# A decoder trunk step on one core: the samples' attention spread over other stages, and two stored products kept as ready-made high and low parts

## The chip, the cores and the metric

The kernel runs on one core of one Trainium2 chip. The metric is device time in microseconds (us) of one execution. Three runs of the kernel before gave 3073.2 us as their median (3071.1 to 3073.73).

## What is computed

One layer of a hybrid decoder trunk runs over two groups of tokens: a prompt of 2048 tokens and 8 samples with one new token each. Cut to what matters here:

```python
z = rmsnorm(x) @ w_in                 # 1024 -> [pool 512 | q 512 | k 512 | v 512]
mix = concat(pool_mix(z_pool), rmsnorm(diff_attn(q, k, v)))
x = x + mix @ w_out                   # "wo"
h = rmsnorm(x)
s = (h @ wq).reshape(heads) @ mem_k.T / 16      # cross-attention into 256 memory tokens, 4 heads
x = x + (softmax(s) @ mem_v) @ wo               # mem_k = mem @ wk, mem_v = mem @ wv
x = x + conv_ffn(rmsnorm(x))          # 1024 -> 2 x 2816 -> 1024
```

For the prompt the differential attention is causal over its own 2048 tokens. For each sample it runs over 512 past tokens, whose keys and values lie in pages and are fetched by a page table, and over the sample's own token. All data are fp32. The kernel forms products in nearly full precision by splitting an operand into a high part (rounded to the fast matmul type) and a low part (the rest) and adding three matmuls.

## The kernel before

**Products prepared once.** `m_head` (L536) forms M = wq of a head times its memory keys, and `vo_head` (L562) forms VO = memory values of a head times wo, for each of four heads. M and VO go to DRAM (`m_d`, `vo_d`) in fp32: ScalarE (ACT) copies each finished 128x512 bank out of PSUM (L557, L573) and issues its store. Heads 0 and 1 are done at the start, heads 2 and 3 beside the second half of the prompt's attention.

**Chunks.** The prompt goes through in four chunks of 512 tokens (the last with the 8 samples appended). For each chunk `p3_items` (L1249) makes: `ld` (load of the mixed heads), `wo` (output projection), `n2` (norm), `sc_` (cross-attention scores against M, L1291), `vo` (weighted values through VO, L1340), `n3` (norm). Each chunk reads all of M (8 tiles of 512 KB) and all of VO (8 tiles of 512 KB) again as weights.

**Weights.** A `Weight` (L295) is staged in three steps: step 0 allocates a buffer and loads it on SyncE's (SP's) queue, step 1 copies it on ACT into the high part (L307), step 2 subtracts on VectorE (DVE) for the low part (L310). `drive` (L440) walks one list of items in order and, ahead of the item in hand, runs step 0, 1 and 2 for as many weights as `look(a0, a1, a2)` says (and two beyond an item that takes weights).

**Samples.** `sample_items` (L1056) take the samples' queries, keys and scores: rows of q and k (L874), then for each sample a load of its query row on SP (L918), four gathers of keys on GpSimd's (POOL's) queue (L921), two multiplications and two reductions on DVE (L932, L934), and at the end one softmax. `sample_items2` (L1059) take the values: four gathers a sample (L999), a split into high and low (L1009), matmuls `sao` (L1016), and the sum (`sample_o`).

**Other work that is spread by hand.** `sums_items` (L1533) prepares combinations of the up-projection's weights for each of 22 column tiles (loads `ws`, four additions and a split on DVE and ACT, stores to `s_d` on POOL's queue). All SBUF tiles of up to 128x1040 share one pool `H` of 41 buffers, the smaller ones (128x536) one pool `S` of 6.

**Order.** The list `order` (L1918 and on) is written by hand with `weave`, which spreads one list over another by the items' costs. In time its stages are: the start with heads 0 and 1 of M and VO; the input projection of chunks 0 and 1; the first half of the attention beside the input projection of chunks 2 and 3; **the second attention**, beside wo of chunks 0 and 1, heads 2 and 3 of M and VO, n2 and scores of chunk 0; then three **output stages**: (1) vo of chunk 0, scores of chunk 1, wo of chunk 2; (2) vo of chunk 1 and the first half of the scores of chunk 2; (3) the rest up to the scores of chunk 3. Behind these comes the FFN of the four chunks, the first of them woven with vo of chunk 3. The change moves items among these stages; each engine takes its own instructions in order.

The lines around the change:

```python
order += weave(weave(vo[0], n2[1], 0.0, 0.9) + weave(sc_[1], ld[2], 0.5, 1.0) + wo[2], sample_items, 0.03, 0.97)   # L1934
order += weave(vo[1] + sc_[2][:8], merge(n2[2], sample_items2[:-2]) + sample_items2[-2:], 0.0, 0.55)               # L1935
```

Of the kernel before, what the change touches and what calls it, by code (L numbers as in the profile page):

```python
# [20 lines left out]
P = 128  # L21
# [3 lines left out]
KT = 8  # L25
# [23 lines left out]
def tile_trunk_step(ctx: ExitStack, tc: tile.TileContext, a, o):  # L49
# [15 lines left out]
    def St(name, dt=F32):  # L65
        return sp.tile([P, SW], dt, tag="S", name=name)
# [13 lines left out]
    def v3(t, k, n=None):  # L80
        n = n if n is not None else 1024 // k
        return t[:, : k * n].rearrange("p (k n) -> p k n", k=k)
# [4 lines left out]
    def f(ap):  # L87
        return ap.bitcast(F32)
# [87 lines left out]
    m_d = dr.tile([NH, 2, P, 1024], F32, name="m_d")  # L176
    vo_d = dr.tile([KT, P, 8, P], F32, name="vo_d")
# [163 lines left out]

    def cols(name, c0):

        return lambda: Weight(a[name][0, :, c0:c0 + P].rearrange("(k p) n -> p k n", p=P), 8)
# [8 lines left out]
    def dram_tile(src, k):  # L353
        return lambda: Weight(src, k)
# [180 lines left out]

    def m_head(h):  # L536
        def fn(raws):
# [11 lines left out]
            for d2 in range(4):  # L549
                ps = PB("M")  # L550
                for k in range(2):
                    dt = 2 * d2 + k
                    for e in range(2):
                        mm3(ps[:, k * 256:(k + 1) * 256], [z[:, dt * P:(dt + 1) * P] for z in wt[e]],
                            (mk[:, e * 256:(e + 1) * 256], mk[:, 512 + e * 256:512 + (e + 1) * 256]), e == 0, e == 1)
                ms = St("ms")
                S.copy(ms[:, :512], ps)  # L557
                S.dma_start(m_d[h, d2 // 2, :, (d2 % 2) * 512:(d2 % 2 + 1) * 512], ms[:, :512])
                yield
        return fn  # L560

    def vo_head(h):  # L562
        def fn(ws):
            mv = p0["v", h]
            for i in range(2):
                for nh in range(2):
# [5 lines left out]
                    vs_ = St("vos")  # L572
                    S.copy(vs_[:, :512], ps)  # L573
                    S.dma_start(vo_d[nh * 4:(nh + 1) * 4, :, h * 2 + i, :].rearrange("n p d -> p n d"), v3(vs_, 4, P))
# [164 lines left out]
    def k_evac(c, h, view):  # L739
# [3 lines left out]
        V.tensor_copy(kh[:, :CH], kf[:, :CH])  # L743
# [454 lines left out]
    def att_post1(qc, h):  # L1198
        O = att["O", qc, h]
        sq = St("osq")  # L1200
        S.activation(sq[:, :512], O, AF.Square)
        ss = Tn("oss")
        V.tensor_reduce(ss[:, 0:4].rearrange("p (a o) -> p a o", o=1), v3(sq, 4, P), AX.X, ALU.add)
# [6 lines left out]
        V.tensor_tensor(v3(on, 4, P), v3(O, 4, P), bc(r, [P, 4, P], 2), ALU.mult)  # L1210
# [38 lines left out]
    def p3_items(c):  # L1249
# [41 lines left out]
        def scores(h):  # L1291
            def fn(ws):
# [3 lines left out]
                def softmax(t0, ps):  # L1296
# [9 lines left out]
                    V.tensor_tensor(e, e, bc(rc[:, :g], [P, g, 256], 2), ALU.mult)  # L1306
# [69 lines left out]
        else:  # L1376
            n2 = norm(GCROSS, "h2", x1_d[c])
        sc_ = sum([steps([dram_tile(m_d[h, 0].rearrange("p (k n) -> p k n", k=4), 4),
                          dram_tile(m_d[h, 1].rearrange("p (k n) -> p k n", k=4), 4)], scores(h), 11.5, 4)
                   for h in range(NH)], [])  # L1380
        vo_ = [item([], reload, 0, 16.0)] + sum([steps([dram_tile(vo_d[nt], 8)], vo(nt), 5.3, 4) for nt in range(KT)], [])
# [526 lines left out]
    def raw_open(_):  # L1908
# [13 lines left out]
    order += weave(weave(half[12:24] + [item([], pool_prep)] + half[24:-8], sums_items(range(5)), 0.0, 0.6),  # L1922
# [4 lines left out]
    order += weave(weave(late[:-16] + att23[0][:2] + late[-16:-10], att01[1]), sums_items(range(5, 13)), 0.05, 1.0) + att23[0][2:]  # L1927
# [4 lines left out]
                   sums_items(range(13, 16)), 0.0, 0.9)  # L1932
    order += [item([], conv_state), item([], raw_open)]
    order += weave(weave(vo[0], n2[1], 0.0, 0.9) + weave(sc_[1], ld[2], 0.5, 1.0) + wo[2], sample_items, 0.03, 0.97)  # L1934
    order += weave(vo[1] + sc_[2][:8], merge(n2[2], sample_items2[:-2]) + sample_items2[-2:], 0.0, 0.55)  # L1935
    order += weave(weave(sc_[2][8:], ld[3], 0.0, 1.0) + weave(wo[3], n3[0], 0.1, 0.9)
                   + weave(vo[2], n2[3], 0.0, 0.9) + weave(sc_[3], xop_items(0) + vo[3][:1], 0.0, 0.85), sums_items(range(16, NF)), 0.0, 0.75)
# [36 lines left out]
```

## Time and profile before

| | |
|---|---|
| median of three runs | 3073.2 us |
| the profiled execution, its own time | 3072.26 us |
| its span, first to last instruction | 3070.5 us |
| TensorE (PE) busy | 2934.5 us, 96% |
| VectorE (DVE) busy | 2243.7 us, 73% |
| ScalarE (ACT) busy | 1353.3 us, 44% |
| GpSimd (POOL) busy | 459.7 us, 15% |
| mean granted TensorE clock | 0.982 of full speed |
| DMA | 683.17 MB, mean 222 GB/s |

PE is the busiest engine all through. What can move the span are the stretches in which it stands still, and those in which its clock is granted at half (1.2 GHz where 2.4 GHz is full speed). A window of the trace gives both: its length less PE's busy time, and the mean granted clock (PEclk) of it.

### The profile page before, as it was taken

To read this page: it belongs to the slowest core of one execution; us is meant where nothing else is said; L and a number is where in the kernel's file an instruction comes from. 1 tells how busy PE (TensorE), PEld (TensorE's weight loads), DVE (VectorE), ACT (ScalarE), POOL (GpSimd) and SP (SyncE) were. 2 spreads that over 40 slices of the span, in tenths; PEclk is the share of its full clock that TensorE was granted. 3 is DMA by queue.
4 is the path that set the end of the run, shared out by engine and by line. 5 is a ranking of instruction groups with operands and counts; after the bars stand their busy time and mean duration, and the time that the engine had idled before them with its cause. 6 is when DMAs were issued, how large, how long until landed. Compare 5 with 4: busy or idle time off the path is not lost.

```text
span 3070.5 us, 52699 instructions
## 1 busy us (share of the span) xinstructions
PE 2934.5 (96%) x19806; PEld 2644.1 (86%) x19806; DVE 2243.7 (73%) x4168; ACT 1353.3 (44%) x2271; POOL 459.7 (15%) x865
## 2 busy tenths in 40 slices
PE   7999999999999889899999999999999999999998
PEld 6789889978888779598888899888898989899998
DVE  5745777667767577667768978888788777877777
ACT  4544455455656424343443344434444433443333
POOL 0244224200000041611100000010000010000000
PEclk9999999999999999999999999999999999999999
DMA  8797578654554467668579876777767686576762
GB/s 277 231 299 244 168 248 272 203 181 143 163 165 128 132 201 235 191 222 307 191 229 337 279 258 192 262 244 243 248 226 259 218 277 211 173 268 221 242 207 103
DMA packets 522627, 683.17 MB, mean 222 GB/s; under 512 B 29585, under 2 KB 344472, under 8 KB 522356
## 3 DMA queue, kind: packets, MB, share of 16 engines
q1 hardware_dynamic: 468637, 533.88, 53.9%
q0 software_dynamic: 39936, 135.17, 12.6%
q10 hardware_dynamic: 13798, 10.76, 1.1%
q8 instruction: 156, 2.56, 0.3%
q14 instruction: 100, 0.81, 0.1%
HBM read 549.12 MB, written 130.98 MB: 221 GB/s over the span
## 4 chain that ended last, share of the span: by engine, by line
PE 60%; DVE 6%; DMA 3%; issue 2%; ACT 2%; POOL 1%; SPq 0%; DVEq 0%; ACTq 0%; POOLq 0%
PE up L1640 15%; PE down L1756 15%; PE up L1642 7%; PE wo L487 4%; PE upB L1640 2%; PE S L99 2%; PE S L100 2%; PE S L101 2%; PE O L1175 1%; PE upB L1642 1%; PE vo L101 1%; PE vo L99 1%; PE vo L100 1%; DMA vg<-in_cache_v_dram,idx 1%; PE sc L1122 1%
## 5 line engine op out<-in xcount | busy, mean ns | idle before, releaser
L1756 PE MATMUL down<-act,whi 128*128 128x512 f32 (+1 forms) x1760 | 450.0, 350 | 0.2 <-DVE xf L1760 0.2
L1640 PE MATMUL up<-xhi,shl 128*128 128x256 f32 (+1 forms) x2816 | 405.5, 285 | 8.7 <-DVE s L1645 4.6
L1640 PEld LDWEIGHTS up<-xhi,shl 128*128 128x128 f32 x2816 | 365.5, 188 | 37.5 <-ACT s L1655 14.3
L1694 ACT ACTIVATE cc<-Uf,vec 128x512 f32<-128x512 f32 (+1 forms) x176 | 144.0, 818 | 494.7 <-DVE Uf L1645 476.9
L310 DVE TENSOR_TENSOR wlo<-wraw,whi 128x1024 fp32r<-128x1024 f32 x256 | 309.8, 1218 | 42.4 <-ACT whi L307 35.7
L1756 PEld LDWEIGHTS down<-act,whi 128*128 128x128 f32 x1760 | 285.5, 188 | 32.7 <-DVE xf L1760 1.5
L307 ACT CAST whi<-wraw 128x1024 fp32r<-128x1024 f32 x256 | 265.6, 1046 | 81.7 <-DMA wraw<-in_w_down_dram 22.6
L1756 PE MATMUL down<-act,wlo 128*128 128x512 f32 (+1 forms) x880 | 279.9, 350 | 1.9 <-DVE wlo L310 1.9
L1699 POOL COPY halo<-Uf 128x2 f32<-128x2 f32 x176 | 60.1, 342 | 1321.9 <-DVE Uf L1645 1300.2
L1642 PE MATMUL up<-xlo,shl 128*128 128x256 f32 (+1 forms) x1408 | 223.7, 281 | 0.0
L1140 ACT ACTIVATE T<-T,mn 128x1024 f32<-128x1024 f32 (+4 forms) x192 | 172.0, 897 | 103.2 <-DVE mn L1133 102.4
L1640 PE MATMUL up<-xhi,whl 128*128 128x256 f32 (+1 forms) x1408 | 199.4, 284 | 6.1 <-DVE whl L329 4.6
L1122 PE MATMUL sc<-K,Q 128*128 128x512 f32 (+5 forms) x640 | 172.5, 388 | 25.3 <-DVE mn L1133 25.1
L1640 PEld LDWEIGHTS up<-xhi,whl 128*128 128x128 f32 x1408 | 184.1, 189 | 14.6 <-DVE whl L329 5.8
L1642 PEld LDWEIGHTS up<-xlo,shl 128*128 128x128 f32 x1408 | 191.1, 188 | 0.3
L1702 DVE SCALAR_TENSOR_TENSOR cc<-Uf,vec,cc 128x512 f32<-128x512 f32 x176 | 131.5, 747 | 73.8 <-ACT cc L1694 70.2
L329 DVE TENSOR_TENSOR whl<-wraw,whl 128x512 fp32r<-128x512 f32 x264 | 178.0, 682 | 1.5 <-ACT whl L327 1.5
L1756 PEld LDWEIGHTS down<-act,wlo 128*128 128x128 f32 x880 | 153.7, 188 | 24.8 <-DVE wlo L310 3.5
L1760 DVE TENSOR_TENSOR xf<-xf,down 128x512 f32<-128x512 f32 (+1 forms) x240 | 134.8, 577 | 55.1 <-PE down L1756 53.9
L1645 DVE TENSOR_TENSOR Uf<-up,s 128x256 f32<-128x256 f32 (+1 forms) x264 | 111.4, 422 | 81.2 <-PE up L1642 78.9
L327 ACT CAST whl<-wraw 128x512 fp32r<-128x512 f32 x264 | 154.9, 615 | 30.4 <-PE up L1642 14.8
L1133 DVE CUSTOM_DVE_ANT_0 T<-sc,Dt 128x1024 f32<-128x1024 f32 (+7 forms) x128 | 125.8, 985 | 44.4 <-PE sc L1122 40.5
(434 smaller groups left out, 7068.1 us busy)
## 6 DMA issues: line engine op xcount, KB each, us to landing
shl<-s_d SPq DMA_DIRECT2D x352, 512.0 KB
wraw<-in_w_up_dram SPq DMA_DIRECT2D x264, 256.0 KB
wraw<-in_w_down_dram SPq DMA_DIRECT2D x88, 512.0 KB
ws<-in_w_up_dram SPq DMA_DIRECT2D x176, 128.0 KB
s_d<-shi POOLq DMA_DIRECT2D x44, 512.0 KB, 4.7
s_d<-slo POOLq DMA_DIRECT2D x44, 512.0 KB, 6.7
wraw<-in_w_in_dram SPq DMA_DIRECT2D x32, 512.0 KB
Q<-q_d SPq DMA_DIRECT2D x64, 256.0 KB
```

The costliest lines, as they stand in the source:

```text
L307: S.copy(self.hi[:, :1024], self.raw[:, :1024])
L310: V.tensor_tensor(self.lo[:, :1024], self.raw[:, :1024], f(self.hi[:, :1024]), ALU.subtract)
L327: S.copy(self.hl[:, :512], self.raw)
L329: V.tensor_tensor(self.hl[:, 512:1024], self.raw, f(self.hl[:, :512]), ALU.subtract)
L1122: PE.matmul(ps[:, j * 512:j * 512 + w], v3(Q[c], 2)[:, z, self.t * P:(self.t + 1) * P], K[c][hf][:, c0:c0 + w], start=z == 0, stop=z == 1)
L1140: S.activation(tg[:, :mg], tg[:, :mg], AF.Exp, bias=mn[:, last:last + 1], scale=-1.0, accum_out=self.l[:, 2 * g + c:2 * g + c + 1])
L1640: PE.matmul(out, wi[:, k, :], xh[:, k], start=k == 0 and wi is wl, stop=False)
L1642: PE.matmul(out, wh[:, k, :], xl[:, k], start=False, stop=k == 3)
L1694: S.activation(cc[:, :w], U[:, 2:2 + w], AF.Identity, bias=vc(CB + nt), scale=vc(CWT + 2 * FT + nt))
L1702: V.scalar_tensor_tensor(cc[:, :CH], U[:, 1:1 + CH], vc(CWT + FT + nt), cc[:, :CH], ALU.mult, ALU.add)
L1756: PE.matmul(out, st["w"][0][wi][:, p, n0:n0 + P], act[:, z + c0:z + c0 + n], start=st_ and p == 0, stop=en and p == g - 1)
L1760: V.tensor_tensor(xx[:, c0:c0 + n], xx[:, c0:c0 + n], out, ALU.add)
```

## The change

1. **Stages of the samples.** `sample_items` (keys, scores, softmax) move from output stage 1 to the second attention, merged with the weight sums of four column tiles; they begin after a pause of 25 units of that list. `sample_items2` (values) move from output stage 2 to output stage 1 (chunk 0's vo, chunk 1's scores, chunk 2's wo), spread over nearly all of it.
2. **Weight sums** are dealt out anew: 7, 7, 4 and 4 column tiles in the four stages that had 5, 8, 3 and 6.
3. **M and VO** are stored as high and low parts. The writer splits each bank (ACT the high part, DVE the low part, both from PSUM) and ACT issues two stores. The reader, `Parts`, loads both parts on SP's queue at staging step 2, with no work on ACT or DVE.
4. **DVE work to ACT.** In `k_evac` the rounding of k; in `att_post1` the squares' sums (four ACT instructions with their accumulator for one square and a DVE reduction) and the scaling of the output (four ACT instructions for one of DVE); in `scores` the softmax's division (one ACT instruction for each 256 columns, for one of DVE).

```diff
-    m_d = dr.tile([NH, 2, P, 1024], F32, name="m_d")
-    vo_d = dr.tile([KT, P, 8, P], F32, name="vo_d")
+    m_d = dr.tile([NH, 2, 2, P, 1024], F32, name="m_d")
+    vo_d = dr.tile([2, KT, P, 8, P], F32, name="vo_d")
...
+    class Parts(Weight):
+        def stage(self, n):
+            if n == 2:
+                self.hi, self.lo = H("dhi", F32R), H("dlo", F32R)
+                for t, src in zip((self.hi, self.lo), self.src):
+                    SY.dma_start(f(v3(t, self.k)), src)
...
+    def parts_out(ps, dst, k=1):
+        hi, lo = St("ph", F32R), St("pl", F32R)
+        split(hi[:, :512], lo[:, :512], ps)
+        for t, d in zip((hi, lo), dst):
+            S.dma_start(d, f(t[:, :512] if k == 1 else v3(t, k, 512 // k)))
...
-                ms = St("ms")
-                S.copy(ms[:, :512], ps)
-                S.dma_start(m_d[h, d2 // 2, :, ...], ms[:, :512])
+                parts_out(ps, [m_d[h, d2 // 2, z, :, ...] for z in range(2)])
...
-        V.tensor_copy(kh[:, :CH], kf[:, :CH])
+        S.copy(kh[:, :CH], kf[:, :CH])
...
-        S.activation(sq[:, :512], O, AF.Square)
-        V.tensor_reduce(ss[:, 0:4]..., v3(sq, 4, P), AX.X, ALU.add)
+        for t in range(4):
+            S.activation(sq[:, t * P:(t + 1) * P], O[:, t * P:(t + 1) * P], AF.Square, accum_out=ss[:, t:t + 1])
...
-        V.tensor_tensor(v3(on, 4, P), v3(O, 4, P), bc(r, [P, 4, P], 2), ALU.mult)
+        for t in range(4):
+            S.activation(on[:, t * P:(t + 1) * P], O[:, t * P:(t + 1) * P], AF.Copy, scale=r[:, t:t + 1])
...
-                    V.tensor_tensor(e, e, bc(rc[:, :g], [P, g, 256], 2), ALU.mult)
+                    for j in range(g):
+                        S.activation(e[:, j], e[:, j], AF.Copy, scale=rc[:, j:j + 1])
...
-                   ... sums_items(range(5)), 0.0, 0.6),
+                   ... sums_items(range(7)), 0.0, 0.6),
...
-    order += weave(weave(late ..., att01[1]), sums_items(range(5, 13)), 0.05, 1.0) + att23[0][2:]
+    order += weave(weave(late ..., att01[1]), sums_items(range(7, 14)), 0.05, 1.0) + att23[0][2:]
...
     order += weave(weave(att23[1], late[-10:] + ld[0] + wo[0] + weave(p0_items((2, 3)), n2[0], 0.0, 0.5)
                          + sc_[0] + ld[1] + wo[1], 0.0, 1.0),
-                   sums_items(range(13, 16)), 0.0, 0.9)
+                   merge(sums_items(range(14, 18)), [item([], lambda _: None, 0, 25.0)] + sample_items), 0.0, 0.95)
...
-    order += weave(weave(vo[0], ...) + weave(sc_[1], ...) + wo[2], sample_items, 0.03, 0.97)
-    order += weave(vo[1] + sc_[2][:8], merge(n2[2], sample_items2[:-2]) + sample_items2[-2:], 0.0, 0.55)
+    order += weave(weave(vo[0], ...) + weave(sc_[1], ...) + wo[2], sample_items2, 0.03, 0.97)
+    order += weave(vo[1] + sc_[2][:8], n2[2], 0.0, 0.55)
...
-                   + ..., sums_items(range(16, NF)), 0.0, 0.75)
+                   + ..., sums_items(range(18, NF)), 0.0, 0.75)
```

## Rows read from the trace of the kernel before

**Rows 1.** The page, busy time of each engine: us, share of the span, instructions.
```profile
PE 2934.5 (96%) x19806; PEld 2644.1 (86%) x19806; DVE 2243.7 (73%) x4168; ACT 1353.3 (44%) x2271; POOL 459.7 (15%) x865
```
**Rows 2.** Windows by stage: length, busy us of the engines, PEclk, DMA share, GB/s.
```profile
0.00:112.00 112.00, 89.07 (x551) 77.88 (x552) 67.09 (x122) 63.11 (x104) 11.66 (x53) 0.92 0.75 254
112.00:295.00 183.00, 183.00 (x1040) 157.92 (x1038) 102.68 (x166) 79.95 (x124) 82.41 (x129) 1.00 0.81 268
295.00:650.00 355.00, 333.28 (x2265) 301.87 (x2265) 253.39 (x591) 187.46 (x374) 101.45 (x159) 0.97 0.71 223
650.00:1083.00 433.00, 405.13 (x2651) 357.26 (x2650) 288.52 (x550) 242.28 (x461) 17.98 (x25) 0.97 0.47 147
1083.00:1239.00 156.00, 147.63 (x857) 128.39 (x856) 122.08 (x215) 50.28 (x88) 48.36 (x49) 0.98 0.65 215
1239.00:1314.00 75.00, 65.43 (x281) 42.42 (x280) 51.59 (x81) 29.87 (x30) 51.36 (x36) 0.91 0.66 206
1314.00:1532.00 218.00, 203.29 (x1448) 190.21 (x1447) 152.83 (x243) 85.76 (x149) 28.68 (x36) 0.97 0.72 242
1532.00:1640.00 108.00, 107.32 (x695) 94.41 (x694) 69.37 (x106) 46.15 (x73) 6.33 (x24) 1.00 0.78 257
```
**Rows 3.** Waits of PE, 1083:1239: total us, times, longest.
```profile
PE oT L1217 <- DVE on L1210: 4.2, 1, 4.2
PE R L257 <- DVE ri L207: 3.2, 1, 3.2
```
**Rows 4.** Waits of PE, 1239:1314.
```profile
PE sao L1016 <- ACT vh L94: 6.6, 2, 3.8
```
**Rows 5.** Waits of PE, 1314:1532.
```profile
PE vo L101 <- DVE wlo L310: 6.1, 3, 3.7
PE S L99 <- DVE wlo L310: 3.9, 2, 3.3
PE stat L250 <- DVE h2sq L232: 3.0, 1, 3.0
```
**Rows 6.** The page, costliest groups: busy us, mean ns of one | idle before.
```profile
L310 DVE TENSOR_TENSOR wlo<-wraw,whi 128x1024 fp32r<-128x1024 f32 x256 | 309.8, 1218 | 42.4 <-ACT whi L307 35.7
L307 ACT CAST whi<-wraw 128x1024 fp32r<-128x1024 f32 x256 | 265.6, 1046 | 81.7 <-DMA wraw<-in_w_down_dram 22.6
```
**Rows 7.** Groups by line, DVE, 1083:1240.
```profile
L932 DVE TENSOR_TENSOR kg<-kg,qb 128x1024 f32<-128x1024 f32 x16 | 19.4, 1220 | 8.2 <-DMA kg<-in_cache_k_dram,idx 8.1
L934 DVE TENSOR_REDUCE sr<-kg 128x16 f32<-128x1024 f32 x16 | 19.0, 1207 | 0.0
```
**Rows 8.** Groups by line, DVE, 650:1083.
```profile
L95 DVE TENSOR_TENSOR wqlo<-wqT,wqhi 128x512 fp32r<-128x512 f32 x8 | 5.1, 683 | 0.4 <-ACT wqhi L94 0.4
L1210 DVE TENSOR_TENSOR on<-O,ry 128x512 f32<-128x512 f32 x6 | 4.1, 689 | 0.1
```
**Rows 9.** Groups by line, ACT, 650:1083.
```profile
L1304 ACT ACTIVATE E<-S,nbx 128x256 f32<-128x256 f32 x16 | 7.4, 472 | 5.3 <-DVE nbx L1299 4.9 <-DVE rt L191 0.4
```
**Rows 10.** Windows inside the second attention, and one of output stage 1; columns as in Rows 2.
```profile
740.00:760.00 20.00, 16.64 (x112) 14.35 (x113) 19.10 (x34) 13.69 (x27) 0.00 (x0) 1.00 0.32 106
760.00:940.00 180.00, 168.09 (x1206) 153.09 (x1205) 128.78 (x247) 112.11 (x216) 7.20 (x9) 0.97 0.51 161
...
1140.00:1200.00 60.00, 59.02 (x456) 56.73 (x455) 57.36 (x80) 27.14 (x55) 15.12 (x13) 1.00 0.80 259
```
**Rows 11.** Waits of PE, 650:1083.
```profile
PE sc L1122 <- DVE mn L1133: 16.1, 12, 4.2
```
**Rows 12.** Waits of DVE, 650:1083.
```profile
DVE T L1133 <- PE sc L1122: 29.7, 21, 4.9
```
**Rows 13.** Waits of SP's DMA queue, 1083:1239.
```profile
SPq L918 <- DVE sal L937: 51.4, 5, 13.3
SPq L918 <- DMA qs_d<-za: 13.5, 1, 13.5
```
**Rows 14.** The page, DMA queue of SP: packets, MB, share of 16 engines' span.
```profile
q1 hardware_dynamic: 468637, 533.88, 53.9%
```

More of the change, by code (lines that the diff above doesn't have):

```diff
@@ L353, in dram_tile @@
     def dram_tile(src, k):
-        return lambda: Weight(src, k)
+        return lambda: Parts(src, k)
     def item(specs, fn, cost=0.0, lat=0.0):
@@ L555, in fn @@
                             (mk[:, e * 256:(e + 1) * 256], mk[:, 512 + e * 256:512 + (e + 1) * 256]), e == 0, e == 1)
-                ms = St("ms")
-                S.copy(ms[:, :512], ps)
-                S.dma_start(m_d[h, d2 // 2, :, (d2 % 2) * 512:(d2 % 2 + 1) * 512], ms[:, :512])
+                parts_out(ps, [m_d[h, d2 // 2, z, :, (d2 % 2) * 512:(d2 % 2 + 1) * 512] for z in range(2)])
                 yield
@@ L571, in fn @@
                         mm3(ps[:, :512], l, r, e == 0, e == 1)
-                    vs_ = St("vos")
-                    S.copy(vs_[:, :512], ps)
-                    S.dma_start(vo_d[nh * 4:(nh + 1) * 4, :, h * 2 + i, :].rearrange("n p d -> p n d"), v3(vs_, 4, P))
+                    parts_out(ps, [vo_d[z, nh * 4:(nh + 1) * 4, :, h * 2 + i, :].rearrange("n p d -> p n d")
+                                   for z in range(2)], 4)
                     yield
@@ L1377, in p3_items @@
             n2 = norm(GCROSS, "h2", x1_d[c])
[L1378 to L1381, printed above, removed]
+        sc_ = sum([steps([dram_tile([m_d[h, i, z].rearrange("p (k n) -> p k n", k=4) for z in range(2)], 4)
+                          for i in range(2)], scores(h), 11.5, 4) for h in range(NH)], [])
+        vo_ = [item([], reload, 0, 16.0)] + sum([steps([dram_tile([vo_d[z, nt] for z in range(2)], 8)], vo(nt), 5.3, 4) for nt in range(KT)], [])
         vo_ += [item([], spill(x2_d))]
@@ L1921, in tile_trunk_step @@
     order += [look(3, 2, 1)]
-    order += weave(weave(half[12:24] + [item([], pool_prep)] + half[24:-8], sums_items(range(5)), 0.0, 0.6),
+    order += weave(weave(half[12:24] + [item([], pool_prep)] + half[24:-8], sums_items(range(7)), 0.0, 0.6),
                    n1[2][0] + n1[2][1] + n1[3][0] + n1[3][1][:5] + [item([], att_table)], 0.65, 1.0)
@@ L1926, in tile_trunk_step @@
     order += [look(4, 3, 2)]
-    order += weave(weave(late[:-16] + att23[0][:2] + late[-16:-10], att01[1]), sums_items(range(5, 13)), 0.05, 1.0) + att23[0][2:]
+    order += weave(weave(late[:-16] + att23[0][:2] + late[-16:-10], att01[1]), sums_items(range(7, 14)), 0.05, 1.0) + att23[0][2:]
     p3 = [p3_items(c) for c in range(NCH)]
```

8 lines of the change are left out of this document (3 added, 5 removed).

## Prediction

> **What bounds the kernel now.** First the page's busy times: PE works 96% of the span, DVE 73%, ACT 44% [rows 1]. So no engine's sum of work is worth counting unless it shortens PE's standstills. Next the windows by stage [rows 2]; the reader is to subtract PE's busy time from each length and look at PEclk. The input projection (112 to 295) has nothing to give: 183.00 of 183.00 us busy at full clock. The FFN's beginning (1532 to 1640) has 0.7 us. What stands still is the start (22.9 us), the first attention (21.7), the second attention (433.00 - 405.13 = 27.9), and the three output stages (8.4, 9.6 and 14.7, together 32.7). The clock takes more: a stretch at half clock does half the work, so (1 - PEclk) x length is lost beside the idle time: 13.0 us in the second attention, and 3.1, 6.8 and 6.5 = 16.4 in the output stages. PEclk is below 1.00 only in stages in which PE stands still; I take it that a removed wait takes its share of half clock with it. The last view is who ended PE's waits there [rows 3 to 5]: in the output stages nearly all are DVE or ACT late with a preparation. The change reaches 32.7 + 16.4 = 49 us there and 40.9 in the second attention.
>
> All sums are made against the profiled execution (3072.26 us, of which 3070.5 are span), 0.9 us under the median of the runs shown; I add the 0.9 at the end.
>
> **The change part by part.**
>
> *M and VO as parts, reading.* Each of four chunks reads 16 such tiles: 64 times one ACT copy of 1046 ns and one DVE subtraction of 1218 ns go [rows 6], 67 us of ACT and 78 us of DVE; 48 of the 64 lie in the output stages, 8 at the end of the second attention, 8 in the FFN. The gain is what waited for them: PE waited 6.1 us before vo and 3.9 before the scores for these subtractions [rows 5]. Next late there is the DMA. Added are 64 loads of 512 KB. By SP's queue as a whole, 533.88 MB in 53.9% of the span [rows 14], that is 533.88 MB / 1655 us = 323 GB/s, so 1.6 us of all 16 engines each: 48 x 1.6 = 78 us in 449 us of output stages, whose DMA is 0.65 to 0.72 busy [rows 2]. Two column tiles of sums leave them (each some 1 MB in and 2 MB out: 20 us together), as do 8 MB of keys (26 us), the values stay in them. Net +32 us of 449, 7 points: the share goes to about 0.76, below the 0.81 that the input projection bears with PE never idle. I cost this DMA at nothing; if its cover goes, it costs at most those 32 us.
>
> *Their lead.* The raw load was issued at staging step 0, the parts' loads are at step 2, in order on SP's queue behind newer loads. Beside the FFN the look-ahead is (6, 3, 2), so a load issued up to six weights ahead now comes two ahead. The 8 VO tiles of chunk 3 share the 108 us window of the FFN's beginning [rows 2], 13.5 us each, in which about three FFN items take a weight too: two weights are some 7 us. Two loads in turn take 3.2 us of full DMA plus their start. Bounds: 0, and 8 x 1.6 = 13 us if one load of each pair is late. I take +2, since the window's DMA share is 0.78.
>
> *M and VO as parts, writing.* 32 banks: ACT's copy stays, a DVE subtraction from PSUM comes (683 ns [rows 8]), and a second store on ACT's queue. That store waits for DVE; behind it stand ACT's next PSUM copies and exponentials, for which PE waits. PSUM banks and two of the six small buffers are held longer. 16 banks are in the start (10.9 us more DVE on 67.1 of 112 [rows 2]), where PE already stands still for preparation, 16 in the second attention. Bounds for the start: 0, and 16 x 0.683 = 11 us with no cover. I take +3, as DVE there is 60% busy.
>
> *Values into output stage 1.* In stage 2 PE stood 6.6 us for the values' high parts [rows 4]: eight samples' gathers run through 75 us, with POOL busy 51 [rows 2]. Spread over 156 us each gather has twice the time. These 6.6 go, and of the rest of the stage's 9.6 idle and 6.8 clock most was in the same places: I take -13 of 16.4. POOL's gathers now stand in order among stage 1's stores of x as the keys' did. New in stage 1 is 16 x 1.2 us of DVE splits against 16 x (1.22 + 1.21) = 39 us of keys that leave [rows 7]; 16 weight subtractions (19 us) leave as well.
>
> *Output stage 1 itself.* The 4.2 us for the last head's output and the 3.2 us for a norm's chain of short DVE instructions [rows 3] were spent behind the samples' rows, keys and weight subtractions on DVE, all of which go. With their 3.1 us of clock that is 10.5; 3 come back for the values' first matmuls: -7.
>
> *Output stage 3.* 6.1 + 3.9 = 10 us of waits go, with two thirds of the 6.5 us of clock: 14.4. The 3.0 us for the sum of squares [rows 5] stays, being a store and reload of x, and will grow as PE reaches it sooner; I put back 3: -11.
>
> *Keys, scores and softmax into the second attention.* The 25-unit pause and the softmax's tail put the scores at about 760 to 940 of the old time. There DVE works 128.8 of 180 us [rows 10]. It gets 39 us of multiplications and reductions [rows 7], 5 of small ones, 11 of M and VO's low parts, 2 of sums; it loses 8 subtractions (9.8), the division (6 x 0.69, the size of L1210's row) and the two large instructions of three heads' ends (4.1) [rows 6, 8]: 128.8 + 57 - 18 = 168, 93% of the time. The scores of each block wait for DVE (16.1 us [rows 11]), but DVE waits as long for them (29.7 [rows 12]). Bounds: 1140 to 1200 shows DVE 57.36 of 60 with PE 59.02 of 60, so 0; 740 to 760 shows DVE 19.10 of 20 with PE 16.64 [rows 10], 17% idle, against the present 11.9 us idle in 180: 180 x 0.17 - 12 = +18, and half as much again for clock: +27. I take +11, nearer to 0 than to 27, because the items fill DVE's gaps as well as its queue. On SP the queries' loads waited 51.4 + 13.5 us for their buffers and for the stored row [rows 13], and every weight behind them; that wait moves along, into a stage whose weights change slowly. POOL's 32 gathers now precede the attention's stores. The keys hold up to four of 41 large buffers; parts need two per weight where it was three.
>
> *DVE work to ACT.* Division: ACT gets 64 instructions of 256 columns, at most 472 ns each [rows 9], 30 us; the heads' ends 128 instructions of 128 columns, at most the same, 60 us, less 16 squares; k 16 copies. DVE sheds some 45 us. In the second attention ACT is 242.28 of 433 us busy [rows 2], in the output stages far less, so ACT covers it. In the first attention it costs between +5 and -5, as one column tile of sums leaves and ACT's order gets longer: -1. Two more column tiles in the input projection meet a DMA at 0.81: +1, at most +5.
> The Trainium skill, ScalarE: Activation LUTs (Rules for kernel authors), says multiplications belong on VectorE, and gives an ACTIVATE a fixed time to which each per-partition operand adds. By that rule four scalings of 128 columns cost clearly more than the one DVE instruction of 689 ns they replace; the sum would get ACT's bursts at the heads' ends, priced as a rival below.
>
> Sum: -7 - 13 - 11 + 11 + 3 + 2 + 1 - 1 = -15, 3072.3 - 15 + 0.9 = 3058.
>
> **The rivals.**
>
> *DVE bounds the second attention.* If DVE can't be filled beyond what a chain through PE, DVE and ACT allows, the stretch lengthens to 168 us divided by that share. The output stages' gain less the small costs (31 - 5 = 26) is gone at 168 / 206 = 82%: below this the kernel is slower. At 76% it is 221 - 180 = +41 us: 3073 - 26 + 41 = 3088. For it: DVE now stands 29.7 us waiting for scores [rows 12]; 72% is all it does there. Against: 95% in 740 to 760 [rows 10].
>
> *It hides wholly.* If 1140 to 1200 is the pattern, the second attention loses nothing, perhaps gains from ACT's help: -26 to -36, 3042.
>
> *The waits return.* x's reloads and the heavier DMA take the places of the removed preparation waits, so that only the gather's wait and the two of stage 1 go (-14) while the attention takes 11 and the start 3: 3073.
>
> *ACT's bursts.* Each of 16 heads' ends puts 8 x 0.47 - 0.59 = 3.2 us on ACT, ahead of the copies PE waits for. If 1.5 us of each reaches PE: +24, which leaves 3072 to 3082. For it: in 760 to 940 ACT is 112 of 180 us busy [rows 10]; against: that leaves it 68.
> This last is what the rule of the Trainium skill (ScalarE: Activation LUTs, Rules for kernel authors) would make of the time; the trace of before has no such instruction to judge it by.
>
> **How the numbers follow.** Forecast 0.42; hides wholly 0.22; waits return 0.13; DVE bounds 0.15; ACT's bursts 0.08, half of them slower. No change here means within 0.2%, 6 us either side. Faster 0.64, same 0.17, slower 0.19. Range 3030 to 3085: the low end is the wholly hidden case with 12 us more from the first attention and the start, the high end the DVE rival nearly whole. The forecast's own range is 3046 to 3068.
>
> **What would show it.** After: the waits of sao for vh and of vo and S for wlo gone, the stages behind the second attention some 30 us shorter together; DVE above 90% in the middle of the second attention, with more waits of sc for DVE's minimum; the waits before stat still there. The prediction fails if the second attention is over 26 us longer, if PE waits there for ACT's copies instead, or if PE waits for the parts' loads.

## The result, and the profile after

The changed kernel takes 3098.6 us (median of four runs, 3094.5 to 3100.6) against 3073.5 for the kernel before on the same chip (3071.1 to 3076.7): ratio 1.0085, 95% interval 1.0070 to 1.0101. It is slower by 25 us; forecast were 15 us less, and the range ended at 3085. Its profiled execution took 3097.4 us, 3095.7 of them span.

The page after, busy time of each engine, against [rows 1]: DVE gave up 94 us, ACT took nothing on balance, and PE has the same 19806 matmuls.

```profile
PE 2944.7 (95%) x19806; PEld 2655.4 (86%) x19806; DVE 2149.3 (69%) x4068; ACT 1351.8 (44%) x2463; POOL 440.7 (14%) x865
```

The windows after, by the same stages, against [rows 2] (length, busy PE, PEld, DVE, ACT, POOL, then PEclk, DMA share, GB/s). In order: start; input projection in two rows; first attention; second attention; output stage 1; the rest of the output stages in three; the FFN's beginning.

```profile
0.00:126.00 126.00, 93.11 (x550) 81.31 (x551) 75.55 (x135) 62.44 (x103) 11.85 (x52) 0.93 0.74 250
126.00:268.00 142.00, 136.09 (x600) 110.28 (x599) 90.81 (x149) 64.08 (x95) 65.74 (x103) 0.96 0.94 312
268.00:321.00 53.00, 52.89 (x439) 51.68 (x438) 20.34 (x32) 24.85 (x41) 22.51 (x35) 1.00 0.66 228
321.00:686.00 365.00, 336.75 (x2270) 303.47 (x2269) 237.21 (x559) 204.31 (x481) 96.96 (x155) 0.97 0.66 209
686.00:1159.00 473.00, 420.38 (x2687) 369.10 (x2685) 321.28 (x630) 252.19 (x542) 58.73 (x69) 0.95 0.59 185
1159.00:1319.00 160.00, 159.64 (x914) 130.84 (x914) 82.37 (x155) 56.53 (x108) 43.62 (x41) 1.00 0.78 262
1319.00:1364.00 45.00, 45.00 (x202) 36.64 (x201) 19.23 (x34) 5.84 (x6) 2.73 (x4) 1.00 0.81 278
1364.00:1462.00 98.00, 97.42 (x819) 96.99 (x818) 53.15 (x88) 39.43 (x78) 9.65 (x12) 1.00 0.73 241
1462.00:1556.00 94.00, 93.49 (x608) 84.51 (x607) 52.54 (x93) 33.50 (x72) 10.66 (x15) 1.00 0.85 315
1556.00:1664.00 108.00, 107.39 (x694) 94.34 (x694) 59.34 (x97) 39.99 (x69) 6.61 (x24) 1.00 0.87 301
```

The reader is to subtract again. The output stages (1159 to 1556) are full: 1.4 us idle in 397, clock 1.00 throughout. Of the 32.7 us of idle time 31 are gone, and all of the half clock, more than forecast. Everything ahead of them is longer: PE stands 32.9 us in the start (22.9 before), 5.9 in the input projection (0 before), 28.2 in the first attention (21.7), 52.6 in the second (27.9), at PEclk 0.95 there (0.97).

The waits of PE after, second attention (total us, times, longest). The scores wait for DVE's minima as before [rows 11]; new are DVE's chain at a head's end (oss), banks that DVE has not yet subtracted out of (wT for pl), and ACT's copy memtok.

```profile
PE sc L1134 <- DVE mn L1145: 16.8, 16, 3.2
PE sc L1134 <- DVE oss L1217: 7.8, 2, 4.8
PE wT L1176 <- DVE pl L95: 5.5, 3, 2.4
PE wT L1176 <- DVE mn L1145: 4.7, 1, 4.7
PE memkvT L538 <- ACT memtok L531: 4.0, 1, 4.0
```

The same view, 1159:1556: the waits of [rows 3 to 5] are gone, stat's too; this is all that is left over 0.2 us.

```profile
PE wo L496 <- DVE mixlo L95: 0.6, 1, 0.6
PE vo L101 <- DMA dlo<-vo_d: 0.5, 1, 0.5
PE sao L1028 <- DVE vl L95: 0.3, 1, 0.3
```

The same view of the start, 0:126.

```profile
PE wqT L559 <- DVE wqlo L95: 6.7, 1, 6.7
PE memT L512 <- DMA mem<-in_mem_prompt_dram: 5.5, 2, 4.8
PE pool L99 <- DVE plo L95: 4.4, 1, 4.4
PE memkv L99 <- DVE wlo L310: 3.5, 1, 3.5
PE VO L99 <- DVE pl L95: 3.1, 1, 3.1
```

Why DVE is late there: its own waits, 60:90, and then ACT's. The loads of lambda's vectors (`lambda_`, 32 KB each) stand on ACT's queue; ACT came to them 9 us later than before (76.4 against 67.1 us), and every DVE instruction behind stood 6.3 us.

```profile
DVE lp L146 <- DMA lq<-in_lam_k_dram: 6.3, 1, 6.3
```
```profile
ACT whi L307 <- DVE pl L95: 3.6, 1, 3.6
ACT whi L307 <- DMA lq<-in_lam_q_dram: 3.5, 1, 3.5
```

### The profile page after: what moved, and what is told of

Read it like the earlier page. It is cut to its first block, busy times and chain, and to the rows that moved or that the text cites. A ratio compares the mean times of both kernels' runs of the same rounds, so it can differ in the third digit from the quotient of the medians.

```text
span 3095.7 us, 52981 instructions
## 1 busy us (share of the span) xinstructions
PE 2944.7 (95%) x19806; PEld 2655.4 (86%) x19806; DVE 2149.3 (69%) x4068; ACT 1351.8 (44%) x2463; POOL 440.7 (14%) x865
## 4 chain that ended last, share of the span: by engine, by line
PE 55%; issue 9%; DVE 6%; DMA 2%; ACT 2%; POOL 1%; SPq 0%; DVEq 0%; POOLq 0%; ACTq 0%
PE up L1652 15%; PE down L1768 14%; PE up L1654 7%; PE upB L1652 2%; PE S L99 1%; PE S L100 1%; PE S L101 1%; PE vo L99 1%; PE vo L101 1%; PE wo L496 1%; PE vo L100 1%; PE upB L1654 1%; PE O L1187 1%; PE sc L1134 1%; DVE T L1145 1%
## 5 line engine op out<-in xcount | busy, mean ns | idle before, releaser
L1768 PEld LDWEIGHTS down<-act,whi 128*128 128x128 f32 x1760 | 285.4, 188 | 32.7 <-DVE xf L1772 1.6
L310 DVE TENSOR_TENSOR wlo<-wraw,whi 128x1024 fp32r<-128x1024 f32 x192 | 232.9, 1219 | 32.5 <-ACT whi L307 25.5
L307 ACT CAST whi<-wraw 128x1024 fp32r<-128x1024 f32 x192 | 200.1, 1045 | 64.1 <-DMA wraw<-in_w_down_dram 27.2
L1134 PE MATMUL sc<-K,Q 128*128 128x512 f32 (+5 forms) x640 | 179.2, 398 | 35.7 <-DVE mn L1145 27.7
L1134 PEld LDWEIGHTS sc<-K,Q 128*128 128x128 f32 x640 | 114.1, 200 | 60.0 <-DVE mn L1145 38.1
```

What stands on the lines that cost most here:

```text
L307: S.copy(self.hi[:, :1024], self.raw[:, :1024])
L310: V.tensor_tensor(self.lo[:, :1024], self.raw[:, :1024], f(self.hi[:, :1024]), ALU.subtract)
L1134: PE.matmul(ps[:, j * 512:j * 512 + w], v3(Q[c], 2)[:, z, self.t * P:(self.t + 1) * P], K[c][hf][:, c0:c0 + w], start=z == 0, stop=z == 1)
L1768: PE.matmul(out, st["w"][0][wi][:, p, n0:n0 + P], act[:, z + c0:z + c0 + n], start=st_ and p == 0, stop=en and p == g - 1)
```

## The experiments

Since the chips' medians of before lie between 3071 and 3075, kernels are compared by their ratios to it (0.001 is 3.1 us; each interval is 0.0009 to 0.0023 either side). Lengths of stages in us, from the first matmul of one stage to that of the next, from one profiled execution of each kernel, rounded. "Output" is the three output stages together and ends at the first vo matmul of chunk 3, some 12 us into the FFN (the windows above end before these 12 us); "rest" is what follows:

```
             start  input proj.  1st att.  2nd att.  output  rest   ratio [95% interval]
before         112    129+53       355       433      462    1526   1
after          128    140+53       365       471      410    1527   1.0085 [1.0070, 1.0101]
no_parts       111    144+53       364       447      415    1525   0.9969 [0.9958, 0.9981]
parts_only     128    129+53       356       436      455    1526   1.0043 [1.0026, 1.0060]
no_move        127    130+53       368       433      452    1527   1.0067 [1.0051, 1.0084]
no_act         130    139+53       362       480      415    1526   1.0112 [1.0095, 1.0129]
parts_h        124    147+53       365       468      411    1528   1.0065 [1.0042, 1.0087]
store_pool     124    137+53       365       473      410    1526   1.0063 [1.0041, 1.0085]
qb_h           128    140+53       365       478      412    1527   1.0115 [1.0098, 1.0133]
np_sub         116    144+53       367       464      415    1525   1.0040 [1.0025, 1.0054]
np_sub_sb      117    146+53       362       457      415    1525   1.0012 [1.0003, 1.0022]
np_store2      122    140+53       365       454      414    1526   1.0018 [1.0008, 1.0027]
np_store2s     118    143+53       362       454      413    1526   0.9997 [0.9986, 1.0009]
np_write       129    138+53       367       474      413    1526   1.0098 [1.0075, 1.0120]
bank_pool      124    147+53       364       475      411    1526   1.0081 [1.0062, 1.0100]
after_lam      122    139+53       365       470      411    1527   1.0078 [1.0061, 1.0094]
np_sums        112    130+53       368       447      413    1526   0.9937 [0.9920, 0.9954]
np_post1       113    129+53       359       450      415    1527   0.9924 [0.9904, 0.9944]
np_soft        112    130+53       369       447      414    1525   0.9929 [0.9910, 0.9947]
np_mix         114    129+53       367       452      415    1526   0.9954 [0.9938, 0.9971]
```

**Which part of the change it is.** Four kernels: the change without the parts (M and VO stored and read whole), the parts alone on the kernel before, the change in the order of before, and the change with DVE's work back.

```diff
 no_parts:    parts_out(...), Parts(src, k)  ->  S.copy + one store, Weight(src, k)
 parts_only:  before.py with parts_out and Parts, nothing else
 no_move:     sample_items, sample_items2, sums_items(range(...)) as in before.py
 no_act:      V.tensor_copy(kh), V.tensor_reduce(ss), V.tensor_tensor(on), V.tensor_tensor(e) as in before.py
```

> The changed kernel, with M and VO kept in fp32 as before (written by one ACT copy and one store, read by load, ACT copy and DVE subtraction); the move of the samples, the sums' deal and DVE's work on ACT stay. Theory W (the writing of the parts holds PSUM banks until DVE's subtraction and puts a store that waits for DVE on ACT's queue): the start returns to 112 us (-14), the second attention gets some 15 to 20 us shorter, while the output stages lose their preparation for vo and scores, some 15 to 20 us longer: 3075 to 3090 in all, start at 112. Rival S (the samples' keys fill DVE in the second attention): the second attention stays at 465 to 475 us, the start still returns or not, total 3100 or more.

> The kernel before with the parts alone. Theory W: start at some 124 us (+12), the second attention +15, the output stages some 25 us shorter: 3070 to 3080. Rival S: start and second attention within 5 us of before, output stages shorter by 25: 3045 to 3055.

> The changed kernel with the hand-written order of before: samples' keys and values and the weight sums in their old stages; parts and DVE's work on ACT stay. Theory W: start stays at some 126 us, the second attention stays 15 to 20 us above its 434 of before, the input projection's first 142 us go back to some 131 as the two column tiles of sums leave; the output stages keep most of their gain but for the waits for the values: 3085 to 3095. Rival S: the second attention returns to 434 or so, total 3065 to 3075.

> The changed kernel with the rounding of k, the heads' ends and the softmax's division back on DVE. Rival A (ACT's longer order delays the copies that PE waits for): the first attention goes from 365 to about 354, the second loses some 10 us, total 3075 to 3080. Theories W and S: within 6 us of the changed kernel, 3092 to 3105.

Without the parts the change is faster than before. The start's 15 us are the parts' alone (111 without, 128 with them alone). The input projection's 11 to 15 are the order's. The output stages' gain is the order's too: 47 of 51 us come without the parts, 6 come with the parts alone. In the second attention the moves with ACT's help cost 13 us and the parts in the old order 3, yet all together 38: what the parts do there depends on what stands beside them. ACT's help is worth 8 us in that stage and costs 3 in the first attention; in the old order (no_move against parts_only) it is worth 4 and costs 12. Neither theory fits all four runs: W wanted a longer second attention in no_move, which has the 433 of before, and S a second attention that stays long in no_parts, which has 447.

**The small buffers and the stores' engine.** Theory B: the parts and the samples compete for the six small buffers. Theory W1: ACT waits at its second store for DVE.

```diff
 parts_h:     hi, lo = St("ph"), St("pl")  ->  hl = H("phl"); hi, lo = hl[:, :512], hl[:, 512:1024]
 store_pool:  parts_out: S.dma_start(d, ...)  ->  G.dma_start(d, ...)
 qb_h:        qb = St("qb")  ->  H("qb")
```

> After, with the high and low part of each bank of M and VO in one large buffer (of 41) in place of two of the six small ones. Theory B (the parts and the samples' query rows and scalings compete for the six small buffers): the second attention, 473 us in after, falls to about 450 (it is 447 without the parts), and the start by some 5 of its 15 us; in all about 3070. Rival W (the bank itself is held until DVE has subtracted, and ACT's second store waits for DVE with ACT's next copies behind it): buffers change nothing; second attention 465 to 475, start 125 to 128 us, in all 3094 to 3100. A third way: a large buffer more in use delays weight loads, and the second attention gets longer, up to 480.

> After, with the parts' two stores issued by POOL in place of ACT, so that ACT never waits for DVE's subtraction. Theory W1 (ACT waiting at the second store is what holds PE): start back from 127 to 115 us, second attention from 473 to about 455, in all about 3070. Rival W2 (the PSUM bank held until the subtraction): start 123 to 128, second attention 465 to 475, in all about 3095. Against the gain: on POOL the stores stand in order with the samples' gathers, whose rows wait for banks; if that holds the parts' buffers, the second attention is over 480.

> After, with the samples' spread query rows in a large buffer in place of one of the six small ones. Theory B (small buffers short): the second attention falls from 473 by 10 to 25 us, the start stays at 127, in all 3075 to 3088. Rival (no shortage of small buffers there): within 3 us of after.

Neither is it. The start gives back 4 us, the second attention 4 or nothing, and the rows' large buffer did not help (478). In parts_h the input projection takes more than the start gave back (147 against 140). With POOL issuing both stores the gathers share POOL's queue with them, and DVE stands 10.1 us for keys in the second attention against 2.1 in the changed kernel, so this run doesn't rule out that ACT's issue costs something; it rules out that it is the whole.

**The writing taken apart.** On the change without the parts, DVE's subtraction out of each bank alone, a second store alone, both; and the parts with DVE out of them. The cuts show M; VO is treated alike.

```diff
 np_sub:     + ml = St("ml"); V.tensor_tensor(ml[:, :512], ps, ms[:, :512], ALU.subtract)
 np_store2:  + S.dma_start(m2_d[...], ms[:, :512])
 np_write:   + ml = ...; V.tensor_tensor(...); S.dma_start(m2_d[...], ml[:, :512])
 bank_pool:  parts_out: S.copy(x, ps); G.tensor_copy(hi, x); G.tensor_tensor(lo, x, f(hi), ALU.subtract); G.dma_start x2
```

> The new order and ACT's work, M and VO kept and read whole, and one thing of the parts' writing put back: DVE's subtraction out of each bank, into a small buffer that nothing reads. Against the same kernel without it (start 111, second attention 447, in all 3061). Theory W2 (the bank is held until DVE has come to it): start 118 to 125, second attention 458 to 470, in all 3080 to 3093. Rival (the second store is the cost): start 111 to 114, second attention 447 to 451, in all 3061 to 3068.

> The same base, with only a second store of each of M's and VO's tiles, from the same small buffer to other memory, and no subtraction. Rival to W2 (the store's bytes, its turn on ACT's queue and the longer hold of the small buffer): start 118 to 125, second attention 455 to 470, in all 3075 to 3093. By theory W2 the stores alone cost little: start 111 to 114, second attention 447 to 452, in all 3061 to 3068.

> The same base, with the whole writing of the parts (subtraction and its own store, to memory that nothing reads), while M and VO are still read whole and split on arrival. If writing is the parts' whole cost and reading saves as little as the runs so far say, start 127, second attention 471, output stages as without the parts, in all 3098 to 3104. If the reading of the parts is what slows the second attention, that stays below 460 here, in all under 3085.

> After, with DVE out of the parts' writing: ACT copies the bank to a small buffer and frees it, POOL rounds the high part, subtracts the low one and issues both stores. Theory W2: start back at 111 to 115, second attention 447 to 455, in all 3055 to 3070. Rival (the bytes of the second store, or the reading): start 120 to 128, second attention 465 to 475, in all 3085 to 3100. Against both: POOL is slow at 512 columns, and if its two operations take 3 us and more each the small buffers are short, so that the start gets longer than 128.

Both theories were half right. The subtraction costs 5 us in the start and 17 in the second attention, the second store 11 and 7; together they come to 18 and 27 in np_write. By the ratios, 0.0071 and 0.0049 add to 0.0120, and np_write stands 0.0129 above no_parts, 40 us: 18 and 27 are more than that because the input projection behind the start is 6 us shorter there (138 against 144). Writing is the whole price as far as can be told: np_write, which still reads M and VO whole, and the changed kernel, which reads parts, are 4 us apart (1.0098 and 1.0085), with some 8 us of uncertainty by their intervals.

In the start the subtraction's 5 us are not a longer standstill. PE stands 23.2 us with it and 23.4 without; its matmuls take 5 us more, at a lower granted clock. The same stretch of np_sub and of no_parts:

```profile
0.00:116.00 116.00, 92.83 (x553) 81.73 (x553) 75.30 (x135) 63.15 (x104) 11.05 (x52) 0.93 0.73 244
```
```profile
0.00:111.00 111.00, 87.61 (x552) 76.86 (x553) 67.63 (x122) 63.32 (x104) 11.88 (x53) 0.97 0.77 257
```

PE's waits in np_sub, 681:1148, show the banks (wT for ml), and a longer wait of the scores for DVE; in no_parts (672:1119) the row with ml is absent.

```profile
PE sc L1126 <- DVE mn L1137: 15.9, 15, 2.5
PE sc L1126 <- DVE oss L1209: 8.3, 2, 5.4
PE wT L1168 <- DVE ml L559: 4.8, 2, 2.6
```
```profile
PE sc L1122 <- DVE mn L1133: 11.3, 15, 1.7
PE sc L1122 <- DVE oss L1205: 8.0, 2, 5.1
```

bank_pool's second attention did not come back (475), and its trace shows costs of its own. Groups of DVE instructions in 679:1159, of the changed kernel and then of bank_pool (busy us, mean ns | idle before): the two-input multiplication on SBUF got longer, the one-input reduction did not. Three of the sixteen multiplications, those that ran beside POOL's rounding or subtraction, took 1559, 3345 and 1625 ns; the other thirteen took 1204 to 1226.

```profile
L944 DVE TENSOR_TENSOR kg<-kg,qb 128x1024 f32<-128x1024 f32 x16 | 19.5, 1221 | 9.4 <-issue 5.6 <-DMA kg<-in_cache_k_dram,idx 2.1 <-DMA qb<-qs_d 1.7
L946 DVE TENSOR_REDUCE sr<-kg 128x16 f32<-128x1024 f32 x16 | 19.0, 1213 | 5.4 <-ACT wT L1178 3.2 <-PE O L1187 2.2
```
```profile
L947 DVE TENSOR_TENSOR kg<-kg,qb 128x1024 f32<-128x1024 f32 x16 | 22.4, 1400 | 16.5 <-DMA kg<-in_cache_k_dram,idx 16.1 <-issue 0.5
L949 DVE TENSOR_REDUCE sr<-kg 128x16 f32<-128x1024 f32 x16 | 19.0, 1212 | 9.2 <-PE O L1190 4.0 <-ACT wT L1181 3.4 <-PE oT L1232 1.9
```

DVE also stood 16.1 us for the gathers, which share POOL's queue with the new work (2.1 in the changed kernel). So it says nothing about the bank; the next run was made for that.

**The bank or the instruction, the bytes or the issue.**

```diff
 np_sub_sb:   V.tensor_tensor(ml, ps, ms, subtract)  ->  V.tensor_tensor(ml, ms, ms, subtract)   (ACT's copy, not the bank)
 np_store2s:  S.dma_start(m2_d[...], ms[:, :512])  ->  S.dma_start(m2_d[..., :16], ms[:, :16])
 after_lam:   lambda_: the four loads of lq at the kernel's start, into a buffer of their own
```

> M and VO kept and read whole, with a subtraction of 512 columns added per bank as in the run with the subtraction alone (start 116, second attention 464, in all 3086), but from ACT's copy in the small buffer, not from the bank: DVE has the same work, and the bank is free when ACT has copied. Its result is not read. If the bank's hold is the cost: start 111 to 113, second attention 447 to 453, in all 3061 to 3070. If DVE's 16 more instructions in its order are the cost: start 115 to 117, second attention 460 to 466, in all 3081 to 3088.

> M and VO kept and read whole, with a second store per bank as in the run with the second store alone (start 122, second attention 454, in all 3078), but of 16 columns: 8 KB in place of 256. If the bytes are the cost (the start's DMA is full from about 50 us on, and the small buffers are held while they go): start 111 to 113, second attention 447 to 449, in all 3061 to 3065. If it is the issue itself and its turn on ACT's queue: start 118 to 122, in all 3071 to 3078.

> After, with the four small loads of lambda's vectors issued at the kernel's start into a buffer of their own, in place of 77 us on, on ACT's queue behind the parts' stores and into one of the six small buffers. DVE stands 6.3 us for them in after, and PE 6.7 us for the DVE instruction behind. If this wait is a part of the parts' price in the start: start 127 falls to 119 to 122, in all 3090 to 3094. If the DMA, full at that time, is the limit behind it: the weight's wait takes its place, start 125 to 128, in all 3095 to 3100.

A DVE instruction of the same size that holds no bank costs 10 of the 17 us in the second attention and 6 us in the start, no less than the one out of the bank; the other 7 of the second attention go with the bank's hold. A store of 8 KB costs the second attention the same 7 us as one of 256 KB, and the start 7 of 11: most of its price is not the bytes. What fits is the issue on ACT's in-order queue. In the second attention the issues of these stores take 5.7 us of ACT's queue in no_parts (16 issues), 14.9 in np_store2s and 16.0 in np_store2 (32 each). M's first and second stores in np_store2s (ns min/median/max):

```profile
L560 ACTq DMA_DIRECT2D m_d<-ms x16: 326/326/1262, 46.5 to 916.1; - x16
L561 ACTq DMA_DIRECT2D m_d<-ms x16: 326/455/975, 46.9 to 916.5; - x16
```

PE's waits in np_sub_sb, 679:1138: the wait for the bank is gone, the scores' wait for DVE stays.

```profile
PE sc L1126 <- DVE mn L1137: 18.2, 19, 2.1
PE sc L1126 <- DVE oss L1209: 6.9, 2, 3.9
```

With lambda's loads issued at once the start is 122 against 128, though PE's waits for the first loads and their preparation (memT, memkv, memkvT) are 1.3 to 1.5 us longer each. PE's waits in after_lam, 0:122: where it stood 6.7 us it stands 1.3, so the late issue acted through these loads. On the whole time the two ratios overlap.

```profile
PE wqT L560 <- DVE wqlo L95: 1.3, 1, 1.3
```

**The order and ACT's work.** Column tiles dealt 5, 9, 4, 4 in place of 7, 7, 4, 4; then the heads' ends, the division, or the ends of heads 0 and 1 alone back on DVE.

```diff
 np_sums:   no_parts with sums_items(range(5)), range(5, 14)
 np_post1:  np_sums with att_post1 as in before.py
 np_soft:   np_sums with V.tensor_tensor(e, e, bc(rc), ALU.mult) as in before.py
 np_mix:    np_sums with att_post1 as in before.py for h < 2
```

> The new order and ACT's work without the parts (M and VO kept whole, as before), and the column tiles of sums dealt 5, 9, 4, 4 over the stages as before's first stage had them, in place of 7, 7, 4, 4. Theory D (the input projection is longer because two more column tiles fill its DMA, 0.94 busy against 0.81): that stage falls from 145 to about 131 us; the first attention takes the two tiles at 5 us or less; in all 3048 to 3054, against 3061 with 7, 7, 4, 4. Rival (the tiles only move, and the first attention's chains pay for them): the first attention 12 us longer, in all 3060.

> M and VO kept whole, sums dealt 5, 9, 4, 4 (first attention 368, second 447, in all 3051), with the ends of the attention's heads (squares, their sum, the scaling by the norm) back on VectorE as before. If ACT's 12 short instructions per head and chunk cost the first attention its length: first attention 358 to 363, second 447 to 450, in all 3042 to 3048. If DVE's two large instructions per end cost more: second attention 452 to 458, in all 3054 to 3060.

> M and VO kept whole, sums dealt 5, 9, 4, 4, with only the cross attention's division back on VectorE. It runs behind the first attention, four heads of one chunk beside the second attention's middle: if this is what the work moved to ACT gains, second attention 451 to 456, output stages 0 to 4 us longer, in all 3055 to 3061. Rival: nothing waits for it there, in all 3049 to 3053.

> M and VO kept whole, sums dealt 5, 9, 4, 4, the ends of heads 0 and 1 (the first attention) on VectorE and those of heads 2 and 3 (the second) on ACT: the better place of each in the runs so far (first attention 359 against 368, second 447 against 450). If the two stages are independent: 3045, 3043 to 3047. If the order of DVE and ACT in the second attention hangs on the first: no gain over 3048.

Two tiles less give the input projection 15 us back (144 to 130); the first attention, which takes them, gets 4 us longer, and the ratio falls by 0.0032, 10 us. At a DMA share of 0.86 PE never stands in the input projection, at 0.90 it stands 11 us. Windows of np_sums, and the same stage of no_parts:

```profile
112.00:242.00 130.00, 129.83 (x599) 105.65 (x598) 78.16 (x126) 58.54 (x90) 58.99 (x93) 1.00 0.86 282
```
```profile
111.00:256.00 145.00, 133.96 (x601) 108.16 (x600) 90.68 (x146) 63.79 (x95) 66.81 (x102) 0.96 0.90 298
```

and DVE's waits in the changed kernel's input projection: a small buffer is still being stored when it is needed (11.6 us for the same in no_parts).

```profile
DVE kl L756 <- DMA out_k_p_dram<-ks: 13.5, 2, 9.5
```

That the DMA is the limit is argued from these rows and not shown by itself: np_sums takes the two tiles' DVE and ACT work away with their bytes, PE's own longest wait in no_parts is for ACT (xT, 7.2 us), and the share alone does not give the standstill (0.94 and 5.9 us in the changed kernel).

The heads' ends back on DVE shorten the first attention by 9 us and lengthen the second by 3, as expected by sign; the division can be on either engine. np_mix does not test what its expectation says, since both attention stages hold all four heads, each of two chunks. Dividing by head leaves 5 of the first attention's 9 ends on DVE and the other 4, 16 scalings, on ACT; in the second it is 4 of 7:

```profile
L1210 ACT ACTIVATE on<-O,ry 128x128 f32<-128x128 f32 x16 | 4.5, 364 | 4.9 <-DVE ry L1207 4.9
L1227 DVE TENSOR_TENSOR on<-O,ry 128x512 f32<-128x512 f32 x5 | 3.5, 690 | 0.2
```

Whether the gains of the two stages add stays open, as does why this mixture is the slowest of the four. np_post1 has the lowest ratio, 0.9924 (0.9904 to 0.9944): faster than both kernels, by 23 us than the one before; from np_sums and np_soft it can't be told.

## Why the prediction was wrong, step by step

- **The step that failed: "M and VO as parts, writing".** It was priced at DVE's time, +3 with bounds 0 and 11, in the start alone; the second attention's 16 banks were 11 us of DVE in a sum that took +11 for everything. Measured: +18 in the start and +27 in the second attention (np_write against no_parts), 40 us by the ratios. The text named the store behind DVE and the banks held longer, and then priced neither. Without the parts the change gains: 0.9969.
- **"Two more sums in the input projection", +1, at most +5:** +11 in the changed kernel, 15 between np_sums and no_parts. The share of 0.81 that I read there [rows 2] is a mean over two parts; the part that takes the tiles had 0.86 and the tail 0.66 (windows of before). At 0.86 the cover was nearly used up.

```profile
112.00:242.00 130.00, 130.00 (x601) 106.13 (x600) 81.86 (x133) 55.77 (x85) 59.66 (x94) 1.00 0.86 283
242.00:295.00 53.00, 53.00 (x442) 51.79 (x440) 20.82 (x33) 24.19 (x40) 22.74 (x35) 1.00 0.66 232
```

- **"DVE work to ACT" in the first attention, -1:** +11, and +9 in no_parts. How much of it is ACT's work hangs on the order: taking all of it back gives 3 us in the changed kernel (no_act), the heads' ends alone 9 in np_post1, all of it 12 in the old order (no_move against parts_only). The rest of the 11 is not explained. Four squares with their accumulator reads and four scalings per head's end are 4 x (0.271 + 0.204 + 0.366) = 3.4 us of ACT in the rows below (groups of ACT, first attention, nine ends), against one 0.6 us square before; the forecast had this as the rival of ACT's bursts, 0.08, with rows from the second attention for it. There ACT's work gains (no_act is 8 us longer, np_post1 3). The Trainium skill, ScalarE: Activation LUTs, Rules for kernel authors, wants multiplications on VectorE. These runs bear it out in the first attention and not in the second.

```profile
L1222 ACT ACTIVATE on<-O,ry 128x128 f32<-128x128 f32 x36 | 10.2, 366 | 8.1 <-DVE ry L1219 7.5 <-DVE rcu L1164 0.6
L1214 ACT ACTIVATE osq<-O 128x128 f32<-128x128 f32 x36 | 9.3, 271 | 2.4 <-PE O L1187 2.4
L1214 ACT ACTIVATION_READ_ACCUMULATOR osq<-O 128x1 f32 x36 | 7.3, 204 | 0.0
```

- **"Keys, scores and softmax into the second attention", +11, bounds 0 and 27:** +13 in no_parts. Right in sign and about in size, but DVE did not fill as I forecast: the middle of that stage has it 86% busy in no_parts and 77% in the changed kernel, where I forecast 93%. These are the rows (windows of no_parts and of the changed kernel):

```profile
770.00:940.00 170.00, 152.60 (x1027) 135.55 (x1026) 146.03 (x280) 110.74 (x231) 27.48 (x27) 0.94 0.62 190
```
```profile
785.00:965.00 180.00, 146.67 (x944) 128.19 (x942) 138.66 (x264) 94.73 (x201) 25.99 (x26) 0.91 0.66 206
```

  The sign of failure that the prediction named for this stage, more than 26 us, came: +38. DVE did not get more to do: over the whole stage it works 322.8 us in no_parts and 321.3 in the changed kernel, as ten weight subtractions leave while sixteen low parts come. The stage got longer under the same work. I read it as a chain through PE, DVE and ACT with each queue in order, in which an instruction ahead of the chain's next link costs its whole length, whether or not the engine is busy on average. This is the rival "DVE bounds the second attention": at a share of 76% it gave +41 there and 3088, and the stage has 77%, +38 and 3098.6. The reading is argued, and two rows bear on it. 16 DVE instructions off every bank cost 10 us (16 x 0.68 = 11), as it wants. But np_write does 13 us more on DVE in this stage than the changed kernel (334.5 against 321.3 us) and is only 2 us longer, so an instruction's price depends on its place in the queue, which no run varied.
- **The output stages, -31:** -51. Nearly all idle time and all half clock went, where I left 18 us. The place was right, the attribution wrong: the 14.4 us of stage 3, waits of vo and S with their clock, were put down to the subtractions of M and VO, and went without the parts too. In no_parts (1119:1522) this is all that PE waits for them, against 10 us before [rows 5]:

```profile
PE S L99 <- DVE wlo L310: 1.8, 1, 1.8
```

  The moves end these waits by themselves; that they do it through fewer samples' rows and sums on DVE is argued. The parts alone end them as well, but gain only 6 us in these stages: in parts_only (1102:1545) a wait for a part's load has come in their place.

```profile
PE vo L99 <- DMA dhi<-vo_d: 6.3, 1, 6.3
```

  One slack was counted for two edits. The 20 us beyond the forecast are luck in the total: at -31 the kernel would have been 45 us slower.
- **"Their lead", +2:** the rest is 1 us longer; right. The loads' bytes cost next to nothing in the changed kernel's output stages, as said (0.5 us of PE's waits), but not in the old order, as the row of parts_only shows.

The stages add up: +15 +11 +11 +38 -51 +1 = +25.

## What to carry to other kernels

A new instruction in a queue that feeds a chain can cost its own length there, even if its engine is a quarter idle; price it at that unless a row shows that nothing of the chain stands behind it, with the DMA's issue and the hold of its bank as terms of their own. Two edits that remove the same wait gain once: ask of each what is left if the other is made alone. A DMA share is to be read over the stretch that receives the work, not over the stage.

## What the runs showed of the hardware

- In the second attention a store of 8 KB that ACT issues cost what one of 256 KB did: 454 us with either, 447 with neither. In the start it cost 7 us against 11.
- POOL's elementwise work slows DVE: three two-input multiplications on SBUF that ran beside it took 1559 to 3345 ns, the thirteen others 1204 to 1226; the mean of the one-input reduction was 1212 ns against 1213. The Trainium skill, Advanced Engine Details and Errata, GPSIMD Details, says that the two share a read and a write interface and conflict where a DVE instruction has two SBUF inputs. The rows agree.
- Half clock does not follow idle time in proportion. In the second attention no_parts has 31.3 us of idle time (the gaps before its matmuls summed) and 39.5 at half clock, np_sub 43.6 and 46.2, np_sub_sb 40.8 and only 35.3. In the start np_sub has as much idle time as no_parts, and a clock of 0.93 against 0.97. So the prediction's share of half clock that goes with each wait held in the output stages and is no rule.
